# Mixed activations staged among the products of the tile ahead; last norms one tile later

## The chip, the cores and the metric

The kernel runs on one core of a Trainium2 chip, as one program. The metric is the device time of one execution in microseconds. A core has five engines that run side by side, each with its own queue in which work is done in order: TensorE (PE, matrix products, with weight loads shown apart as PEld), VectorE (DVE, elementwise work with two operands, reads the product banks), ScalarE (ACT, casts, activations with scale and bias), GpSimd (POOL, elementwise work, and the issue of some DMAs) and SyncE (SP, the issue of the other DMAs). Products land in PSUM banks; the rest of the data lies in SBUF tiles of 128 partitions.

## What is computed

One layer of a hybrid backbone over 17 tiles of 128 tokens (tile 0 the context, tiles 1 to 16 the latent tokens), width 1024, in float32. Cut to what the change touches:

```python
    h = rmsnorm(x, norm1_g) * (1 + scale1) + shift1
    z = h @ w_in
    ...
    mix = jnp.concatenate([o_a, o_b, o_c], axis=-1) @ w_out
    x = x + gate1 * mix
    h = rmsnorm(x, norm2_g) * (1 + scale2) + shift2
    x = x + gate2 * (jnp.square(jax.nn.relu(h @ w_ff1)) @ w_ff2)
    return rmsnorm(x, final_g)
```

o_a is a gated linear attention, o_b a convolution along rows of tokens, o_c a spatial gating.

## The kernel before, in words

Every large product is made as three products of split operands: a float32 value is cast to a short high part on ACT, and the low part is the difference of value and high part, by a subtract on DVE or POOL. `mm3` (L174) then issues high x high, high x low and low x high. One unit of `mm_units` (L134) is three such products of 512 columns for one of eight chunks of the contraction; a tile of the w_out stage has two halves of eight units, 48 products.

The phases in order: the first runs through the tiles upward (w_in, the attention's sums), the second downward from tile 16 (gates, attention output, gating, the convolution's input) and writes each tile's mixed activations to `mix_d[t]` in device memory. Then comes the w_out stage (`out_proj`, L754), from tile 16 down to tile 0. Then the first feed-forward product in two groups of eight latent tiles (`left_operand`, `right_operand`, `ff1_units`), and the second (`ff2_units`, `finish`), which runs over eight chunks of the hidden width and, within each, over the tiles in five blocks.

What `out_proj(t)` does before: it finishes the convolution work that tile t needs (`cq.finish(t)`, L760), takes a buffer `mt` and two for the parts, loads `mix_d[t]` (L766), casts on ACT (L767), subtracts on POOL (L768), loads the residual rows `x1`, and returns the sixteen units. At the end of each half (`done`) DVE multiplies the bank by the gate (L777) and adds the residual (L778); after the second half, POOL stores `x1`, ACT sums the squares (L782), `rstd_of` makes the root (DVE L160, POOL L161) and ACT multiplies (L784). The transposes and the second norm's scaling for that tile (`h2_half`, L797) are handed to the next tile as two items, after its twelfth and its sixteenth unit. For odd tiles `h2_pair` (L815) makes sums and differences of two tiles' results on DVE and stores them to `tb_d` through POOL.

`weave(units, items)` (L149) writes units and items alternately: an item with number n comes ahead of unit n. `ticks` puts one turn of the convolution queue after each unit: `ConvQueue` (L952) holds the tap passes of the convolution (62 for each group of tiles, a DVE pass each), hands them out by a credit of 5.3 a tile, and lists a norm and a silu step per tile as due some slots after the group's last tap. `finish(t)` runs turns at once until what tile t needs is written.

What is written first has the higher priority, but it is no strict order: the planner of the tile framework walks through all instructions when the kernel is built, keeps an estimate of when each is ready and a buffer free, and fixes each engine's queue by that. Products and transposes (`mm`, `tr`), taps and the loads through `ld_in_order` keep the order in which they are written. Buffers come from pools: `T` tiles (18 of 128 x 1024, pool `tp`, opened at L1143 where the buffers `hb` of phase two lay), `w` tiles (23, of which w_out's parts take 16), and for tile 16 the pair of `hunit`.

`right_operand` (L1151) loads one piece of a feed-forward operand from `tb_d`, by a DMA that POOL issues, and splits it in place with ACT and DVE (`split_in_place`, L1147: cast L1148, subtract L1149). It is called for 14 pieces per group of tiles (i from 0 to 6, kk 0 and 1).

In `finish` (L1377), at the last chunk, each half of a tile is multiplied by its gate, added to the residual and squared with a running sum on ACT; after the second half DVE adds the two sums, `rstd_of` makes the root, DVE scales both halves (L1392, recorded at L67) and SP stores them.

Of the kernel before, what the change touches and what calls it, by code (L numbers as in the profile page):

```python
# [8 lines left out]
F32 = mybir.dt.float32  # L9
# [11 lines left out]
NT = 17  # L21
# [22 lines left out]
def tile_hybrid(  # L44
# [12 lines left out]
    def x_rows(t):  # L57
        return x_prompt[0] if t == 0 else x_sample[0, (t - 1) * P:t * P, :]

    def y_rows(t):  # L60
        return y_prompt[0] if t == 0 else y_sample[0, (t - 1) * P:t * P, :]
# [49 lines left out]
    def wtile(dt=F32R):  # L111
        return wp.tile([P, D], dt, tag="w", name="w", bufs=23)

    def hunit():
        return hb.tile([P, 2, D], F32R, name="hb"), hb.tile([P, D], F32, name="hc")
# [15 lines left out]
    def ld_in_order(out, in_):  # L131
        tc.keep_in_program_order(ld.dma_start(out=out, in_=in_))
# [615 lines left out]
    def tunit(dt=F32R):  # L748
        return tp[0].tile([P, D], dt, tag="T", name="T", bufs=18)

    def gate_row(dst, g, cd):
        ld.dma_start(out=dst, in_=gate_d[g, cd:cd + 1].rearrange("o k p -> o (k p)").broadcast_to([P, D]))

    def out_proj(t):  # L754

        cd = 0 if t == 0 else 1
        if cd not in g1rows:
            g1rows[cd] = wtile(F32)
            gate_row(g1rows[cd], 0, cd)
        cq.finish(t)  # L760
        if t == NT - 1:
            hu, mt = hunit()
            mh, ml = hu[:, 0], hu[:, 1]
        else:
            mt, mh, ml = tunit(F32), tunit(), tunit()
        ld_in_order(out=mt, in_=mix_d[t].rearrange("p k t -> p (k t)"))  # L766
        S.copy(out=mh, in_=mt)  # L767
        G.tensor_tensor(out=ml, in0=mt, in1=mh.bitcast(F32), op=ALU.subtract)  # L768
        x1 = wtile(F32)
        ld_in_order(out=x1, in_=x_rows(t))  # L770

        tmp = xp_tile()[:, 0:D] if t == 0 else wtile(F32) if t == NT - 1 else tunit(F32)

        def done(half):
            def f(pz):
                fs = slice(half * 512, (half + 1) * 512)
                V.tensor_tensor(out=tmp[:, fs], in0=pz, in1=g1rows[cd][:, fs], op=ALU.mult)  # L777
                V.tensor_tensor(out=x1[:, fs], in0=tmp[:, fs], in1=x1[:, fs], op=ALU.add)  # L778
                if half == 1:
                    st.dma_start(out=x1_d[t], in_=x1)  # L780
                    ssq = const.tile([P, 1], F32, name="ssq3", bufs=2)
                    act(tmp, x1, AF.Square, accum_out=ssq)  # L782
                    rstd_of(ssq, ssq, D)
                    S.mul(tmp, x1, ssq)  # L784
            return f

        def lhs(k):
            ks = slice(k * P, (k + 1) * P)
            return mh[:, ks], ml[:, ks]

        units = []
        for half in range(2):
            units += mm_units(512, lhs, of_pairs(wo[half]), done(half))

        hs = []

        def h2_half(kq):  # L797
            pt = gbank()
            for kk in range(4):
                k = kq * 4 + kk  # L800
                tr(pt[:, kk * P:(kk + 1) * P], tmp[:, k * P:(k + 1) * P])
            hf = tmp.rearrange("p (k t) -> p k t", k=KD)
            for kk in range(4):
                k = kq * 4 + kk
                act(hf[:, k, :], pt[:, kk * P:(kk + 1) * P], AF.Identity, scale=s2[:, k, cd:cd + 1],
                    bias=modc[:, KD + k, cd:cd + 1])
            ks = slice(kq * 4, kq * 4 + 4)
            if t == 0:
                split(hc[0][:, ks], hc[1][:, ks], hf[:, ks])
            elif kq == 1:  # L810
                h2_pair(t, hf)

        return units, [(12, lambda: h2_half(0)), (16, lambda: h2_half(1))]
# [22 lines left out]
    def ticks(n, rate):  # L836
        return [(p_ + 0.5, lambda: cq.tick(rate / n)) for p_ in range(n)]
# [3 lines left out]
    with ExitStack() as p2:  # L841
# [293 lines left out]
                late = list(zip((8, 6), late2))  # L1135


        units, late3 = out_proj(NT - 1)
        weave(units, late + ticks(16, RATE3))


    hbs.close()
# [1 line left out]
    hc = []  # L1144
    TB = [{}, {}]

    def split_in_place(hi, lo):  # L1147
        S.copy(out=hi, in_=lo.bitcast(F32))  # L1148
        V.tensor_tensor(out=lo, in0=lo.bitcast(F32), in1=hi.bitcast(F32), op=ALU.subtract)  # L1149

    def right_operand(g, i, kk, dst):  # L1151

        unit = tunit if i < 4 else uunit
        hi, lo = unit(), unit()
        st.dma_start(out=lo.bitcast(F32).rearrange("p (k n) -> p k n", k=2), in_=tb_d[g][:, i, 2 * kk:2 * kk + 2])
        split_in_place(hi, lo)
        dst[i, kk] = (hi, lo)

    for t in range(NT - 2, -1, -1):
        units, nxt_late = out_proj(t)  # L1160
        if t == 0:
            hc += [tunit().rearrange("p (k t) -> p k t", k=KD) for _ in range(2)]
        items = late3 + ticks(16, RATE3)
        if t == 2:

            items += [(10 + 4 * kk, lambda kk=kk: right_operand(0, 0, kk, TB[0])) for kk in range(2)]
        weave(units, items)
        late3 = nxt_late
# [196 lines left out]
    def residual(t, y):  # L1365
# [8 lines left out]

        return half

    def finish(t, y):  # L1377

        ssq = const.tile([P, 2], F32, name="ssq4", bufs=4)
        tmp = raw()  # L1380

        def half(h, py):
            fs = slice(h * 512, (h + 1) * 512)
            V.tensor_tensor(out=tmp[:, fs], in0=py, in1=g2rows[min(t, 1)][:, fs], op=ALU.mult)  # L1384
            V.tensor_tensor(out=y[:, fs], in0=y[:, fs], in1=tmp[:, fs], op=ALU.add)  # L1385
            act(tmp[:, fs], y[:, fs], AF.Square, accum_out=ssq[:, h:h + 1])
            if h == 1:
                V.tensor_tensor(out=ssq[:, 0:1], in0=ssq[:, 0:1], in1=ssq[:, 1:2], op=ALU.add)  # L1388
                rstd_of(ssq[:, 0:1], ssq[:, 0:1], D)
                for i in range(2):  # L1390
                    fs = slice(i * 512, (i + 1) * 512)
                    stt(y[:, fs], y[:, fs], ssq[:, 0:1], fgr[:, fs], ALU.mult, ALU.mult)  # L1392
                    ld.dma_start(out=y_rows(t)[:, fs], in_=y[:, fs])

        return half

# [39 lines left out]
    for c in range(NC_):  # L1436
        w2n = []
        if c == NC_ - 2:
            g2rows[0] = tunit(F32)
            gate_row(g2rows[0], 1, 0)  # L1440
        for b in range(5):
            units = ff2_units(c, b, F, w2)
            items = []
            nb, ncx = (b + 1, c) if b < 4 else (0, c + 1)
            if ncx < NC_:
                F, steps = load_f(ncx, nb)
                items += zip((3.5, 9.5) if b < 4 else (0, 1), steps)
            if c + 1 < NC_ and b < 4:
                items.append((14.5, lambda f=(c + 1) * CF + b: w2n.append(load_ff2(f))))
            weave(units, items)  # L1450
        w2 = w2n
    tps.close()


# [27 lines left out]
```

## Time and profile before

| | |
|---|---|
| time, median of 3 runs | 2534.2 us (2531.51 to 2536.76) |
| the profiled execution: its time | 2536.06 us |
| the profiled execution: its span | 2534.3 us |
| PE busy | 2357.0 us, 93% of the span |
| DVE busy | 1500.6 us, 59% |
| ACT busy | 891.2 us, 35% |
| POOL busy | 432.3 us, 17% |
| mean granted TensorE clock | 0.968 of full speed |

The span runs from the first to the last instruction of the profile; the execution's own time also holds what lies around it. Busy shares are means over stages with different limits. A small helper such as `mm` or `act` gives its own line number to all that it issues, so instructions are told apart by their tiles (`out<-in`): products of the w_out stage are `z<-w,T`.

### The profile page before, as it was taken

Reading aid. Unit: us, or ns where it says so; the run is one execution under the profiler, and the core shown is the slowest. Engines: PE = TensorE matmul, PEld = TensorE weight load, DVE = VectorE, ACT = ScalarE, POOL = GpSimd, SP = SyncE. Lnnn points to the kernel's source line nnn. Section 1 sums busy time; section 2 is a strip of 40 time slices with the busy share of each in tenths; the row PEclk is TensorE's granted clock in tenths of the full one; section 3 lists DMA queues with packets and bytes.
Section 4 is the critical chain, followed back from the end, with each engine's and each line's share of the span. In section 5 each row is a group of like instructions: output and inputs, shape, how many; then the busy total and the mean of one; then the engine's idle time right before and its main releaser. Section 6 shows DMA issues by size and latency. Waiting matters only on the chain. (4 is left out here: it accounts for less than half of the span.)

```text
span 2534.3 us, 32290 instructions
## 1 busy us (share of the span) xinstructions
PE 2357.0 (93%) x12402; PEld 1920.9 (76%) x12402; DVE 1500.6 (59%) x2526; ACT 891.2 (35%) x1710; POOL 432.3 (17%) x593
## 2 busy tenths in 40 slices
PE   7999999999977778699999999999999999999996
PEld 5788886777755556478888778887888888888885
DVE  5987755878875663465555666665134344344886
ACT  4666764332434243443332433333321111011132
POOL 2332225444413233300000100000000000000000
PEclk9999999999988888799999999999999999999998
DMA  8655534433433435433222533334032122122442
GB/s 282 227 203 199 201 123 149 129 129 136 140 130 137 144 121 192 162 108 106 104 95 93 205 117 100 106 127 173 31 100 74 48 87 87 38 92 79 137 152 86
DMA packets 145323, 326.26 MB, mean 129 GB/s; under 512 B 13349, under 2 KB 58703, under 8 KB 141584
## 3 DMA queue, kind: packets, MB, share of 16 engines
q1 hardware_dynamic: 110640, 191.73, 23.1%
q0 software_dynamic: 34528, 132.46, 14.6%
q8 instruction: 98, 1.61, 0.3%
q14 instruction: 57, 0.47, 0.1%
HBM read 213.24 MB, written 110.90 MB: 128 GB/s over the span
## 5 line engine op out<-in xcount | busy, mean ns | idle before, releaser
L126 PE MATMUL z<-w,hb 128*128 128x512 f32 (+1 forms) x2438 | 552.1, 372 | 15.2 <-ACT hb L767 10.6
L126 PEld LDWEIGHTS z<-w,hb 128*128 128x128 f32 x2438 | 412.8, 192 | 92.6 <-ACT hb L767 10.8
L126 PE MATMUL z<-v,u 128*128 128x512 f32 x1224 | 304.3, 391 | 7.2 <-ACT u L1148 4.7
L126 PE MATMUL z<-T,v 128*128 128x512 f32 x1152 | 286.9, 401 | 15.6 <-ACT T L1148 6.4
L126 PE MATMUL g<-v,u 128*128 128x512 f32 x1224 | 300.9, 390 | 0.0
L126 PE MATMUL z<-w,T 128*128 128x512 f32 x768 | 213.3, 430 | 75.5 <-ACT T L767 51.4
L126 PEld LDWEIGHTS z<-v,u 128*128 128x128 f32 x1224 | 229.4, 188 | 60.7 <-DVE u L1149 8.5
L126 PEld LDWEIGHTS z<-T,v 128*128 128x128 f32 x1152 | 218.2, 191 | 70.3 <-ACT T L1148 7.7
L126 PE MATMUL z<-u,v 128*128 128x512 f32 x1152 | 269.8, 392 | 0.0
L126 PEld LDWEIGHTS g<-v,u 128*128 128x128 f32 x1224 | 230.8, 189 | 48.3
L1148 ACT CAST u<-u 128x1024 fp32r<-128x1024 f32 (+1 forms) x92 | 85.6, 938 | 484.4 <-DMA u<-f_d 360.7
L126 PEld LDWEIGHTS z<-u,v 128*128 128x128 f32 x1152 | 218.0, 189 | 46.9
L126 PEld LDWEIGHTS z<-w,T 128*128 128x128 f32 x768 | 152.2, 205 | 118.2 <-ACT T L767 53.5
L67 DVE SCALAR_TENSOR_TENSOR cacc<-xp,wd,cacc 128x512 f32<-128x512 f32 (+2 forms) x360 | 226.7, 683 | 0.0
L1149 DVE TENSOR_TENSOR u<-u 128x1024 fp32r<-128x1024 f32 (+1 forms) x92 | 99.1, 1082 | 114.1 <-ACT u L1148 91.3
L161 POOL TENSOR_TENSOR ssq<-ssq,mhalf 128x1 f32<-128x1 f32 x51 | 34.6, 679 | 773.7 <-DVE ssq L160 772.9
L1422 DVE TENSOR_TENSOR T<-z,T 128x512 f32<-128x512 f32 x102 | 70.4, 690 | 135.8 <-PE z L126 135.4
L172 DVE TENSOR_TENSOR v<-raw,v 128x1024 fp32r<-128x1024 f32 x88 | 107.2, 1220 | 64.0 <-PE z L126 60.2
L1422 DVE TENSOR_TENSOR T<-g,T 128x512 f32<-128x512 f32 x102 | 70.3, 689 | 124.9 <-PE g L126 124.9
L172 DVE TENSOR_TENSOR v<-cacc,v 128x1024 fp32r<-128x1024 f32 x64 | 78.3, 1224 | 86.6 <-PE z L126 86.6
L171 ACT CAST v<-raw 128x1024 fp32r<-128x1024 f32 x88 | 92.5, 1052 | 92.1 <-issue 55.4
L126 PE MATMUL z<-u 128*128 128x512 f32 x408 | 115.3, 391 | 0.0
(288 smaller groups left out, 3116.3 us busy)
## 6 DMA issues: line engine op xcount, KB each, us to landing
raw<-in_w_ff_dram SPq DMA_DIRECT2D x96, 512.0 KB
f_d<-xp POOLq DMA_DIRECT2D x64, 512.0 KB, 3.4
u<-f_d SPq DMA_DIRECT2D x64, 512.0 KB
raw<-in_w_mod_dram SPq DMA_DIRECT2D x32, 512.0 KB
hb<-hT_d POOLq DMA_DIRECT2D x15, 1024.0 KB, 5.6
hT_d<-hb POOLq DMA_DIRECT2D x13, 1024.0 KB, 6.8
ss_d<-ss POOLq DMA_DIRECT2D x34, 256.0 KB, 4.0
r<-ss_d SPq DMA_DIRECT2D x34, 256.0 KB
```

The costliest lines, as they stand in the source:

```text
L67: return V.scalar_tensor_tensor(out=out, in0=in0, scalar=scalar, in1=in1, op0=op0, op1=op1)
L126: tc.keep_in_program_order(T.matmul(out, lhsT, rhs, start=start, stop=stop, skip_group_check=read))
L161: G.tensor_tensor(out=out, in0=out, in1=mhalf[:, 0:out.shape[-1]], op=ALU.pow)
L171: order(S.copy(out=hi, in_=src))
L172: order(V.tensor_tensor(out=lo, in0=src, in1=hi.bitcast(F32), op=ALU.subtract))
L1148: S.copy(out=hi, in_=lo.bitcast(F32))
L1149: V.tensor_tensor(out=lo, in0=lo.bitcast(F32), in1=hi.bitcast(F32), op=ALU.subtract)
L1422: V.tensor_tensor(out=ya[t][:, hs], in0=py, in1=ya[t][:, hs], op=ALU.add)
```

## The change

The load, cast and subtract of the mixed tile move out of `out_proj(t)` into `stage(t)`, whose two parts are items among the units of tile t+1: the loads (with `cq.finish(t)`) ahead of unit 1, cast and subtract ahead of unit 7. The low part is made in the loaded buffer, so a tile takes two T buffers for it instead of three. Tiles 16 and 15 take their buffers from `hunit`. `right_operand` gives the subtract of kk = 1 to POOL; kk = 0 stays on DVE. In `finish` the sum of the two halves' squares, the root, the scaling and the stores of a tile are written after the first half of the next tile (after all others for the last).

```diff
+    staged = {}
+    def stage(t):
+        cq.finish(t)
+        if t >= NT - 2:
+            hu, mt = hunit()
+            mh, ml = hu[:, 0], hu[:, 1]
+        else:
+            mh, ml = tunit(), tunit()
+            mt = ml.bitcast(F32)
+        ld_in_order(out=mt, in_=mix_d[t].rearrange("p k t -> p (k t)"))
+        x1 = wtile(F32)
+        ld_in_order(out=x1, in_=x_rows(t))
+        staged[t] = mh, ml, x1
+        def convert():
+            S.copy(out=mh, in_=mt)
+            G.tensor_tensor(out=ml, in0=mt, in1=mh.bitcast(F32), op=ALU.subtract)
+        staged[t, 0] = convert
+    def stages(t):
+        return [(1.0, lambda: stage(t)), (7.0, lambda: staged[t, 0]())] if t >= 0 else []
     def out_proj(t):
...
-        cq.finish(t)
-        if t == NT - 1:
-            hu, mt = hunit()
-            mh, ml = hu[:, 0], hu[:, 1]
-        else:
-            mt, mh, ml = tunit(F32), tunit(), tunit()
-        ld_in_order(out=mt, in_=mix_d[t].rearrange("p k t -> p (k t)"))
-        S.copy(out=mh, in_=mt)
-        G.tensor_tensor(out=ml, in0=mt, in1=mh.bitcast(F32), op=ALU.subtract)
-        x1 = wtile(F32)
-        ld_in_order(out=x1, in_=x_rows(t))
+        mh, ml, x1 = staged[t]
...
+        stage(NT - 1)
+        staged[NT - 1, 0]()
         units, late3 = out_proj(NT - 1)
-        weave(units, late + ticks(16, RATE3))
+        weave(units, late + ticks(16, RATE3) + stages(NT - 2))
...
-    def split_in_place(hi, lo):
+    def split_in_place(hi, lo, eng=V):
         S.copy(out=hi, in_=lo.bitcast(F32))
-        V.tensor_tensor(out=lo, in0=lo.bitcast(F32), in1=hi.bitcast(F32), op=ALU.subtract)
+        eng.tensor_tensor(out=lo, in0=lo.bitcast(F32), in1=hi.bitcast(F32), op=ALU.subtract)
...
-        split_in_place(hi, lo)
+        split_in_place(hi, lo, G if kk else V)
...
-        items = late3 + ticks(16, RATE3)
+        items = late3 + ticks(16, RATE3) + stages(t - 1)
...
+    norms = []
     def finish(t, y):
...
+            if h == 0 and norms:
+                norms.pop()()
             if h == 1:
-                V.tensor_tensor(out=ssq[:, 0:1], in0=ssq[:, 0:1], in1=ssq[:, 1:2], op=ALU.add)
-                rstd_of(ssq[:, 0:1], ssq[:, 0:1], D)
-                for i in range(2):
-                    fs = slice(i * 512, (i + 1) * 512)
-                    stt(y[:, fs], y[:, fs], ssq[:, 0:1], fgr[:, fs], ALU.mult, ALU.mult)
-                    ld.dma_start(out=y_rows(t)[:, fs], in_=y[:, fs])
+                norms.append(norm)
+        def norm():
+            V.tensor_tensor(out=ssq[:, 0:1], in0=ssq[:, 0:1], in1=ssq[:, 1:2], op=ALU.add)
+            rstd_of(ssq[:, 0:1], ssq[:, 0:1], D)
+            for i in range(2):
+                fs = slice(i * 512, (i + 1) * 512)
+                stt(y[:, fs], y[:, fs], ssq[:, 0:1], fgr[:, fs], ALU.mult, ALU.mult)
+                ld.dma_start(out=y_rows(t)[:, fs], in_=y[:, fs])
...
         w2 = w2n
+    norms.pop()()
     tps.close()
```

## Rows read from the trace of the kernel before

**Rows 1.** Windows, pairs of tiles: length; busy PE, PEld, DVE, ACT, POOL; clock.

```profile
761.29:800.24 38.95, 27.83 (x123) 21.63 (x123) 20.78 (x43) 16.84 (x35) 14.69 (x16) 0.85 0.42 149
800.24:836.53 36.29, 28.29 (x118) 21.91 (x118) 21.75 (x37) 15.63 (x33) 12.46 (x13) 0.88 0.36 127
836.53:873.58 37.05, 27.71 (x113) 21.48 (x113) 23.00 (x31) 12.37 (x24) 11.92 (x12) 0.87 0.42 135
873.58:910.43 36.85, 28.00 (x112) 21.62 (x113) 21.96 (x35) 12.37 (x24) 11.48 (x12) 0.87 0.42 136
910.43:948.09 37.66, 27.80 (x124) 21.92 (x124) 24.78 (x72) 17.03 (x36) 14.46 (x18) 0.86 0.34 112
948.09:985.76 37.67, 27.55 (x121) 21.46 (x121) 17.41 (x37) 17.32 (x37) 14.25 (x17) 0.86 0.45 143
...
1021.48:1058.07 36.59, 27.46 (x113) 21.21 (x113) 9.76 (x15) 12.53 (x25) 11.28 (x12) 0.87 0.25 80
```

**Rows 2.** Waits of PE in the stage: us in total, times, longest.

```profile
PE z L126 <- ACT T L767: 51.4, 8, 8.8
PE z L126 <- POOL T L768: 24.1, 15, 2.3
```

**Rows 3.** Timeline of ACT: start, us, engine, line, operation, out<-in.

```profile
871.44 1.15 ACT L784 ACTIVATE T<-w,ssq 128x1024 f32<-128x1024 f32 x1 [1.03 <-POOL ssq L161]
872.50 1.03 ACT L767 CAST T<-T 128x1024 fp32r<-128x1024 f32 x1
```

**Rows 4.** Timeline of PE, one pair of tiles; in brackets the idle time before.

```profile
876.97 10.79 PE L126 MATMUL z<-w,T 128*128 128x512 f32 x34 [2.17 <-POOL T L768]
...
893.22 8.20 PE L126 MATMUL z<-w,T 128*128 128x512 f32 x34 [1.33 <-POOL T L768]
...
904.49 0.60 PE L129 MATMUL g<-ident,T 128*128 128x128 f32 x4
```

**Rows 5.** Windows of the same pair's two tiles; the granted clock is the third last number.

```profile
873.50:888.50 15.00, 12.75 (x43) 9.72 (x43) 7.43 (x8) 0.23 (x2) 3.40 (x3) 0.69 0.47 141
888.50:905.20 16.70, 15.26 (x71) 11.90 (x69) 11.25 (x21) 7.62 (x17) 4.82 (x4) 1.00 0.38 127
```

**Rows 6.** Timelines of PE and DVE at the end.

```profile
2508.40 0.84 PE L126 MATMUL g<-u 128*128 128x512 f32 x3
...
2513.84 0.84 PE L126 MATMUL g<-u 128*128 128x512 f32 x3
...
2521.47 0.68 DVE L1384 TENSOR_TENSOR raw<-g,T 128x512 f32<-128x512 f32 x1
...
2524.77 1.41 DVE L67 SCALAR_TENSOR_TENSOR T<-T,ssq,cacc 128x512 f32<-128x512 f32 x2 [0.75 <-POOL ssq L161]
```

**Rows 7.** Waits of DVE in the last chunk, from 2421 us on.

```profile
DVE T L67 <- POOL ssq L161: 10.1, 16, 0.8
DVE ssq L1388 <- ACT raw L64: 10.0, 15, 0.8
```

**Rows 8.** Waits of DVE in one pair of tiles, 836.53 to 873.58.

```profile
DVE ssq L160 <- ACT T L64: 2.6, 2, 1.3
DVE T L827 <- ACT T L64: 0.8, 1, 0.8
```

**Rows 9.** Timelines of PE and ACT, one norm of the convolution.

```profile
914.41 0.63 PE L129 MATMUL g<-ident,cacc 128*128 128x128 f32 x2
...
916.83 0.56 ACT L64 ACTIVATE raw<-g,mv 128x256 f32<-128x256 f32 x1 [6.45 <-issue]
```

**Rows 10.** Line L1149: durations ns (least, median, most), first and last start.

```profile
L1149 DVE TENSOR_TENSOR T<-T x16: 1214/1224/1226, 1014.1 to 1457.9; 128x1024 fp32r<-128x1024 f32 x16
```

**Rows 11.** Line L1155 (loads by POOL) in the fill, 1055 to 1100.

```profile
DMA to landing us min/median/max: 7.7/12.3/14.4
```

**Rows 12.** Timelines of DVE and POOL, 872 to 877.

```profile
872.70 4.78 DVE L67 SCALAR_TENSOR_TENSOR cacc<-xp,wd,cacc 128x512 f32<-128x512 f32 x3
...
874.57 2.35 POOL L768 TENSOR_TENSOR T<-T 128x1024 fp32r<-128x1024 f32 x1
```

## The prediction

> **What bounds the kernel now.** I read in this order: the slices of the page, where TensorE (PE) is below nine tenths only in the first slice and from the 12th to the 17th; the busy time of each pair of tiles in this second place, the w_out stage; PE's waits there; PE, ACT, POOL and DVE in order of time; then the chain that ended last, which lies on DVE for the final 100 us. Everywhere else PE is close to full, so the change is worth what PE idle time and slow PE time it removes, and the tail.
>
> The w_out stage (tiles 15 to 0) runs from 761.29 to the next stage's first product at 1058.07 [rows 1]. Inside it PE waits for two things only: the cast of the mixed tile (L767, eight times, 51.4 us) and the low part's subtract on POOL (L768, fifteen times, 24.1 us) [rows 2]. The cast waits for no data: it stands in ACT's queue behind the multiply L784 of the tile just finished, and starts as that ends (871.44 + 1.15, then 872.50) [rows 3]. So for every second tile the chain is last product, eviction, square, root, multiply, cast, two products, subtract, rest. A third loss follows: after the wait 34 products took 10.79 us, in the pair's other tile 8.20 us [rows 4]; the granted clock was 0.69 in that stretch, a mix of the levels of 1.2 and 2.4 GHz, and 1.00, the upper one, in the next, where PE had been at work before [rows 5]. Eight times about 2.4 us is 19 us. Together 51 + 24 + 19 = 94 us.
>
> At the end the last products run from 2513.84 to 2514.68, but DVE finishes the last tile only at 2524.77 + 1.41 = 2526.18 [rows 6]. In that last chunk DVE stands still 10.1 us for POOL's power and 10.0 us for ACT's sum of squares, once each per tile [rows 7].
>
> **The change part by part.**
>
> *Mixed tiles staged one tile ahead.* Cast and subtract of tile t-1 are now written after seven of the sixteen units of tile t, so they stand ahead of tile t's second eviction, square and multiply in the queues. Both are ready when the tile's load has landed, and PE needs them some 6 us later. Removed from PE's path: both waits, and the cold clock behind them. What is late next? A tile without waits is 46 products and 8 transposes from 893.22 to 904.49 + 0.60, 11.87 us, plus two products at 0.24: 12.35 us, 24.7 a pair [rows 4]. DVE's work per pair is 20.8, 21.8, 23.0, 22.0, 24.8 and 17.4 us, less in the last two [rows 1]. DVE works in order, and in a pair it also stands 2.6 us for the sum of squares and 0.8 for the pair's first sum [rows 8]; where convolution norms run (pairs 1, 2, 5 and 6) I add 2.2 us, an estimate from the 3.0 us that a norm takes from its transposes at 914.41 to the end of ACT's normalising at 916.83 + 0.56 [rows 9], shared among three engines. That gives DVE 26.4, 27.4, 26.4, 25.4, 30.4 and 23.0. Taking the larger of DVE and PE: 26.4 + 27.4 + 26.4 + 25.4 + 30.4 + 24.7 + 24.7 + 24.7 = 210 us for sixteen tiles. Today it is 296.8 less the 5.5 us between the last transposes and the next stage's first product, which stay: 291.3. To this comes the wait ahead of tile 15, whose start lies 5.8 us after the end of tile 16. So 291.3 + 5.8 - 210 = 87 us. The ceiling, PE alone, is 8 x 24.7 and 4 us of convolution transposes, 202, which is 95 us.
>
> Against that, three small terms. (1) Tile 14's staging is the first to take slots of the new pool `tp` while tile 15 still sits in the old hb buffers. If its slot lies over those, the load waits for tile 15's last product, and its flight (which no row shows alone; taken as up to 5 us), cast and subtract follow: at most 8 us once, otherwise nothing; I take 3. (2) `cq.finish` is called most of a tile sooner. By the queue's own arithmetic (0.662 credits for a tap of four tiles, 5.3 a tile) the taps of tiles 1 to 4 end in tile 8 as before, and only the last two silu steps, of tiles 2 and 1, are forced early, in tile 5, directly behind tile 1's norm: PE can wait the 3.0 us of [rows 9] less the unit between: 0 to 3, taken as 2. (3) Tile 16's load now goes out on SP ahead of the gate row instead of behind it: 0 to 2 us gained, taken as 1. The staged loads are the same two DMAs per tile on SP; behind one that waits for its slot stand only the next loads. Each tile now takes three slots of T instead of four, so slots come free sooner. Sum for the stage: 87 - 3 - 2 + 1 = 83 us.
>
> *Half of right_operand's subtracts to POOL.* Fourteen of them: 1.22 us on DVE [rows 10] becomes 2.35 on POOL (a subtract of this shape, [rows 12]), while DVE does the other half at the same time. One stands in tile 2, six in the fill of the feed-forward stage, seven at its change of group. Where PE waits for just this operand it loses 1.1 us; where it waited behind DVE's queue it gains 1.2. Bounds: 14 x 1.13 = 16 us lost, to 3 us gained; the loads that feed the fill land 12.3 us after issue [rows 11], so most of it is hidden behind them: 2 us lost. POOL's queue also issues these loads; that is the last rival.
>
> The Trainium skill speaks against this part. "SBUF — State Buffer", section "Who interferes with whom", says that a DVE instruction with two SBUF inputs and a GpSimd instruction that reads SBUF exclude each other. The row agrees: three taps took 4.78 us, where three passes of this shape at 0.68 [rows 6] are 2.0, with POOL's subtract inside [rows 12]. By that rule the shift frees no DVE time; what it does to the staged tiles is rival (b), worked out there from the rows.
>
> *Last norms one tile later.* The norm of a tile is now written after the first half of the next, so DVE no longer waits for the square just issued: of 20.1 us of standing [rows 7] half or more goes. DVE's work per tile there is four passes of 0.68, two of one column and 1.41, some 4.5 us, 5.2 with one wait left, against PE's 5.44 (2508.40 to 2513.84) [rows 6], so PE becomes the bound. The last half still has its chain, from 2521.47 to 2526.18, 4.7 us [rows 6]; it can start at 2514.9, or at 2516 if tile 1's norm is just ahead. The end moves from 2526.2 to between 2519.6 and 2520.7: 5.5 to 6.6 us, taken as 5.5. The output's last landing behind it stays.
>
> Sum: 83 - 2 + 5.5 = 86.5 us. The profiled execution took 2536.1 us (span 2534.3), so 2449.6; it lies 0.07% above the median of 2534.2, and I forecast **2449 us**.
>
> **The rivals.** (a) *PE alone is the bound*: DVE fills its standing time with taps, as the planner may order them otherwise. For it: the warm tiles of today run at PE's pace with a full share of taps. Against: waits of 1.3 us for the squares recur in every tile. 95 + 5.5: 2436 us.
> (b) *DVE falls behind through POOL.* From a tile's end to the end of its multiply lie about 5.4 us (the mean wait of 6.4 us [rows 2] less the cast's 1.03 [rows 3]); its transposes stand after twelve units, 8.7 us. If the staged subtract holds the second eviction for 2.35 us [rows 12] and stands ahead of the power on POOL for as long again, this is 10.1 and PE stalls, 1.4 to 2.4 us in each of the 11 tiles where DVE is nearly full: 15 to 26 us. At the upper end 2449 + 26 = 2475 us. For it: DVE's margin is under 1 us a tile. Against: the subtract is ready before the eviction in most tiles.
> (c) *The staging is not early*: the load waits for slots, or the planner leaves the cast behind the multiply. Then only POOL's 24 us go, with the end's 5.5 less 2: 2508 us. Against: ACT has work for less than half the stage, and loads need fewer slots now.
> (d) *Slower*: on POOL each new subtract waits for a cast that waits for a load. If the planner sets it ahead of the next load's issue, loads go one by one: 12.3 us landing [rows 11], 1.03 cast and 2.35, 15.7 us for each of 13 operands, up to 204 us: 2449 + 204 = 2653 us. It decides from six operands on (six times 15.7 is 94, over the 88 gained elsewhere). Against: the issues wait for no data that POOL makes, so they should go first.
>
> **How the numbers follow.** Forecast (2440 to 2460) 0.48, (a) 0.15, (b) 0.25, (c) 0.08, (d) 0.04. The range covers the forecast, (a) and (b), with the unknown ends of the fill (14 more) and of tile 14: 2434 to 2488; (c), (d) and a little stay out. A measurement of this kernel tells about 0.2% (5 us) from no change. Only (d) is slower; a mild form of it, or (c) with the full loss of 16 us, could end near no change. Faster 0.94, same 0.02, slower 0.04.
>
> **What would show it.** Right: no wait of PE for the cast in the stage and few for POOL; a granted clock near 1.00 from tile 15 on; some 215 us from tile 15's first product to the next stage's; DVE's busy share in it over 0.8 up to tile 5; at the end DVE's last pass some 6 us behind PE's last product. Wrong: PE waiting for the new cast or subtract (c); PE waiting for the multiply ahead of the transposes (b); long gaps between POOL's loads of tb_d (d); a stage still over 240 us.

## The result, and the profile after

The changed kernel takes 2472.9 us (median of 4 runs, 2469.2 to 2478.2) against 2533.3 us in the same set: ratio 0.9762, 95% interval 0.9738 to 0.9785. It is faster, by 60 us; the forecast was 2449 us, a gain of 86.5. The four runs fall into two pairs, 2469.2 and 2470.0 us, and 2475.8 and 2478.2 us; the profile is of the 2475.8. The profiled execution has a span of 2474.1 us (2534.3 before), 60.2 us less, and it is this difference that is taken apart here.

The page after, busy time first, then PE and its granted clock in 40 slices:

```profile
PE 2341.6 (95%) x12402; PEld 1913.3 (77%) x12402; DVE 1518.3 (61%) x2512; ACT 890.6 (36%) x1710; POOL 470.2 (19%) x607
...
PE   6999999999989988799999899999999999999996
...
PEclk9999999999989999799999899999999999999998
```

Of the dip of PE from the 12th to the 17th slice there remain the 12th (tile 16's start), the 15th to 17th (the convolution's norm, the stage's end and the fill), none under 7; there is a new one in the 23rd, at the change of group. What PE waits for from tile 16's first product to the first feed-forward products (725 to 990 us: us in total, times, longest):

```profile
PE g L129 <- ACT raw L64: 9.2, 2, 8.8
PE z L126 <- ACT hb L771: 7.5, 1, 7.5
PE g L129 <- ACT T L799: 7.5, 5, 3.0
PE z L126 <- ACT v L171: 5.3, 1, 5.3
PE z L126 <- ACT T L771: 3.6, 1, 3.6
PE z L126 <- POOL hb L772: 1.5, 1, 1.5
PE z L126 <- POOL T L772: 1.5, 1, 1.5
```

The cast (51.4 us before) and the subtract (24.1) of [rows 2] are gone but for one wait each at tile 14; tile 16's own (`hb`), which lie ahead of the windows of [rows 2], stay. New are the waits for the convolution's norm (`raw`) and for the multiply L799 ahead of the transposes. The same waits in PE's timeline (start, us, in brackets the idle time before):

```profile
734.15 1.22 PE L126 MATMUL z<-w,hb 128*128 128x512 f32 x2 [7.53 <-ACT hb L771]
...
767.61 1.22 PE L126 MATMUL z<-w,T 128*128 128x512 f32 x2 [3.60 <-ACT T L771]
770.31 2.08 PE L126 MATMUL z<-w,T 128*128 128x512 f32 x4 [1.48 <-POOL T L772]
...
808.18 1.12 PE L129 MATMUL g<-ident,T 128*128 128x128 f32 x4 [3.00 <-ACT T L799]
...
902.23 0.69 PE L129 MATMUL g<-ident,raw 128*128 128x128 f32 x2 [8.82 <-ACT raw L64]
902.57 9.60 PE L126 MATMUL z<-w,T 128*128 128x512 f32 x33
...
984.09 5.12 PE L126 MATMUL z<-T,v 128*128 128x512 f32 x12 [5.30 <-ACT v L171]
```

Four stretches hold what changed. They are read from the timelines of every run's profile, and the experiments are compared by them too. "Stage" runs from tile 16's first product to the first `z<-T,v`, "fill" from there to the first `g<-v,T` x24, "change" (the change of group) from the start of the last `z<-u,v` block of the first group to the start of the first one of the second, "tail" from the end of PE's last product to the end of DVE's last pass. All four are in us and of one execution each; the times are medians, and each ratio is to the kernel before as measured beside it. In the last two kernels tile 16's first product can't be told from those ahead of it, so their stage is left open.

| kernel | us | ratio to before (95%) | stage | fill | change | tail |
|---|---|---|---|---|---|---|
| before | 2533.3 | | 319.7 | 43.6 | 30.5 | 11.5 |
| the change | 2472.9 | 0.976 (0.974 to 0.979) | 249.9 | 49.6 | 39.2 | 11.6 |
| ro_only | 2547.8 | 1.005 (1.003 to 1.006) | 321.8 | 49.8 | 36.3 | 11.5 |
| ro_dve | 2456.1 | 0.969 (0.968 to 0.970) | 244.3 | 43.6 | 31.6 | 11.7 |
| ro_sp | 2451.7 | 0.967 (0.966 to 0.969) | 247.0 | 39.7 | 31.5 | 11.6 |
| norm_old | 2475.1 | 0.976 (0.975 to 0.977) | 249.2 | 47.9 | 39.0 | 11.4 |
| norm_kept | 2466.1 | 0.973 (0.971 to 0.974) | 247.7 | 48.1 | 40.2 | 6.0 |
| silu_own | 2463.4 | 0.972 (0.970 to 0.973) | 236.7 | 47.8 | 39.8 | 11.5 |
| sub_dve | 2462.6 | 0.971 (0.970 to 0.972) | 238.3 | 49.9 | 40.1 | 11.5 |
| combo | 2445.1 | 0.965 (0.963 to 0.966) | 238.5 | 43.5 | 30.9 | 6.0 |
| combo_sub | 2432.2 | 0.959 (0.958 to 0.961) | 226.2 | 42.8 | 30.9 | 6.0 |
| best_sp | 2417.1 | 0.953 (0.952 to 0.955) | 226.0 | 38.2 | 22.6 | 6.0 |
| best_s16 | 2404.0 | 0.948 (0.947 to 0.950) | | 38.1 | 22.8 | 6.0 |
| best_half | 2415.8 | 0.954 (0.952 to 0.955) | | 39.9 | 32.3 | 6.0 |

For the change: stage 69.8 us shorter and its start 4.2 us earlier (738.35 to 734.15), together 74 against 83 forecast; fill and change 5.9 and 8.7 us longer, 14.6 against 2; tail 0.1 longer against 5.5 shorter; the rest 0.9 better. 74.0 - 14.6 - 0.1 + 0.9 = 60.2.

### The profile page after: what moved, and what is told of

Its sections match the earlier page's. It is cut to its first block, busy times and chain, and to the rows that moved or that the text cites. A ratio compares the mean times of both kernels' runs of the same rounds, so it can differ in the third digit from the quotient of the medians.

```text
span 2474.1 us, 32304 instructions
## 1 busy us (share of the span) xinstructions
PE 2341.6 (95%) x12402; PEld 1913.3 (77%) x12402; DVE 1518.3 (61%) x2512; ACT 890.6 (36%) x1710; POOL 470.2 (19%) x607
## 3 DMA queue, kind: packets, MB, share of 16 engines
q0 software_dynamic: 34528, 132.46, 15.1%
## 4 chain that ended last, share of the span: by engine, by line
PE 62%; DVE 12%; issue 4%; DMA 4%; ACT 3%; POOL 3%; POOLq 0%; SPq 0%; DVEq 0%; ACTq 0%
PE z L126 42%; PE g L126 19%; DVE cacc L67 5%; DMA T<-tb_d 1%; PE g L129 1%; DMA u<-f_d 1%; DVE T L67 1%; DVE u L1166 1%; DVE T L1404 1%; DVE raw L1403 1%; POOL ssq L161 1%; DVE uv L67 1%; DVE w L793 1%; ACT T L64 1%; ACT raw L64 1%
## 5 line engine op out<-in xcount | busy, mean ns | idle before, releaser
L126 PE MATMUL z<-w,hb 128*128 128x512 f32 (+1 forms) x2486 | 563.0, 373 | 13.5 <-ACT hb L771 7.5
L126 PEld LDWEIGHTS z<-w,hb 128*128 128x128 f32 x2486 | 420.8, 192 | 92.9 <-ACT hb L771 7.8
L126 PEld LDWEIGHTS g<-v,u 128*128 128x128 f32 x1224 | 230.5, 188 | 48.1
L67 DVE SCALAR_TENSOR_TENSOR cacc<-xp,wd,cacc 128x512 f32<-128x512 f32 (+2 forms) x360 | 237.6, 713 | 0.0
L126 PE MATMUL z<-w,T 128*128 128x512 f32 x720 | 183.5, 409 | 5.2 <-ACT T L771 3.6
L126 PEld LDWEIGHTS z<-w,T 128*128 128x128 f32 x720 | 136.3, 194 | 35.9 <-ACT T L771 3.8
L1166 DVE TENSOR_TENSOR u<-u 128x1024 fp32r<-128x1024 f32 (+1 forms) x86 | 91.8, 1073 | 102.8 <-ACT u L1165 102.5
```

Of the source, the lines that this page charges most:

```text
L67: return V.scalar_tensor_tensor(out=out, in0=in0, scalar=scalar, in1=in1, op0=op0, op1=op1)
L126: tc.keep_in_program_order(T.matmul(out, lhsT, rhs, start=start, stop=stop, skip_group_check=read))
L1166: eng.tensor_tensor(out=lo, in0=lo.bitcast(F32), in1=hi.bitcast(F32), op=ALU.subtract)
```

## The experiments

Each is the changed kernel with the edit shown, except ro_only, which is the kernel before. The theory formed from the traces: three losses in three places, each in an order of instructions and not in the work itself (for the change of group the last run shows otherwise); the rivals stand with each run.

**Where fill and change of group lose.** In the kernel before, POOL issues the loads of `tb_d` one behind the other (start, us):

```profile
1061.01 0.53 POOL L1155 DMA_DIRECT2D T<-tb_d  x1
1061.53 0.53 POOL L1155 DMA_DIRECT2D u<-tb_d  x1
1062.30 0.53 POOL L1155 DMA_DIRECT2D T<-tb_d  x1 [0.25 <-DMA tb_d<-T]
```

POOL's timeline after:

```profile
987.16 0.53 POOL L1172 DMA_DIRECT2D T<-tb_d  x1
1000.41 2.44 POOL L1166 TENSOR_TENSOR T<-T 128x1024 fp32r<-128x1024 f32 x1 [12.72 <-ACT T L1165]
1002.80 0.57 POOL L1172 DMA_DIRECT2D u<-tb_d  x1
1003.37 0.54 POOL L1172 DMA_DIRECT2D T<-tb_d  x1
1003.92 2.37 POOL L1166 TENSOR_TENSOR u<-u 128x1024 fp32r<-128x1024 f32 x1
1006.23 0.58 POOL L1172 DMA_DIRECT2D u<-tb_d  x1
```

Before, the sixth and seventh issue follow the fifth at once; after, the sixth stands behind a subtract that waits 12.7 us for the cast of an earlier load. But the subtract is also slower on POOL, and DVE stands beside it. Three kernels ask which of these it is, and a fourth, best_half at the end, is needed for the answer.

```diff
 # ro_dve
-        split_in_place(hi, lo, G if kk else V)
+        split_in_place(hi, lo)
```

> The changed kernel with all subtracts of right_operand back on DVE. Theory: in the changed kernel the fill of the first feed-forward stage took 5.9 us more than before (49.5 against 43.6) and the change of group 9.1 us more (48.7 against 39.6), because POOL, which issues these loads, now puts a subtract that waits for its load between two issues, and DVE stands beside POOL's subtract. Then the whole 15 us come back: 2458 us, 0.994 of the changed kernel's 2473. Rival A, the estimate in the prediction: the shift costs 2 us, and the longer fill has another cause (the stage ends earlier relative to the stores to tb_d): 2471 us. Rival B: what costs is the lock of DVE beside POOL in the staged tiles too, then nothing is seen here but the one operand in tile 2: 2472 us.

2456.1 us: fill and change are back at 43.6 and 31.6. The cause is in the shift, not in the staging. The stage is 5.6 us shorter too: 1.7 us were PE's wait at 962.5 for a multiply in tile 2, behind the subtract of the first operand (POOL, 957.88 to 960.30), and 3.3 us are the clock that these two executions met, not the edit (last section).

```diff
 # ro_only, on the kernel before
...
-        split_in_place(hi, lo)
+        split_in_place(hi, lo, G if kk else V)
```

> The kernel before, with nothing of the change but its second part: right_operand's subtract of kk = 1 on POOL. Theory (POOL issues these loads, and a subtract that waits for its own load stands between two issues): the loss at the fill and at the change of group is there without the staging, 6 + 8.7 us, so 2548 us, 1.006 of the kernel before. Rival: it comes only with the staging, which brings the fill closer to the stores of tb_d: 2535 us, no difference. Rival of the prediction: the subtracts are hidden, 2 us: 2536 us.

2547.8 us against 2535.6, ratio 1.0047 (1.0034 to 1.0060): a small difference, but clear of noise. Alone, this part makes the kernel slower by 12 us, 6.2 in the fill and 5.8 at the change.

```diff
 # ro_sp
-        st.dma_start(out=lo.bitcast(F32).rearrange(...), in_=tb_d[g][:, i, 2 * kk:2 * kk + 2])
+        ld.dma_start(out=lo.bitcast(F32).rearrange(...), in_=tb_d[g][:, i, 2 * kk:2 * kk + 2])
```

> The changed kernel, half of right_operand's subtracts on POOL as in the change, but the loads of tb_d issued by SyncE, where no subtract stands ahead of them. It tells the two causes of the 15 us at the fill and at the change of group apart. Theory (the loads wait in POOL's queue behind subtracts that wait for earlier loads): most of it comes back, 2461 us, with a fill of about 45 us and 32 us between the last two product blocks around the change of group. Rival (POOL's subtract is just slower, 2.35 against 1.22 us, and DVE stands beside it): nothing comes back, 2473 us. A third: on SyncE's queue the loads stand behind weight loads that wait for a buffer, and it is slower than 2473.

2451.7 us. POOL has its subtracts as in the change, and still the change of group is back at 31.5 and the fill at 39.7, shorter than before the change: SyncE issues the fill's first two loads at 971.8 and 972.3, ahead of the first feed-forward product at 978.9. It looks as if it had been the queue alone. But what the subtract itself costs is still there, in the timelines of PE, DVE and POOL at the change of group:

```profile
1370.91 2.19 PE L126 MATMUL z<-T,v 128*128 128x512 f32 x6 [2.91 <-DVE T L1166]
1376.79 2.50 PE L126 MATMUL z<-T,v 128*128 128x512 f32 x5 [3.69 <-POOL T L1166]
...
1371.72 5.58 DVE L1228 TENSOR_TENSOR cacc<-raw,cacc 128x512 f32<-128x512 f32 x1
...
1372.09 2.36 POOL L1166 TENSOR_TENSOR u<-u 128x1024 fp32r<-128x1024 f32 x1
1374.40 2.34 POOL L1166 TENSOR_TENSOR T<-T 128x1024 fp32r<-128x1024 f32 x1
```

A DVE pass that takes 0.68 us in the kernel before took 5.58 with two subtracts inside, and PE waited for DVE and then for POOL. So the loads' move to SyncE must have gained something else there, and the kernel before shows what it can be: a store `f_d<-xp` that waits 8.1 us for DVE stands in POOL's queue ahead of the loads, with no subtract on POOL at all.

```profile
1444.17 0.54 POOL L1250 DMA_DIRECT2D f_d<-xp  x1 [8.10 <-DVE xp L67]
1444.70 0.53 POOL L1155 DMA_DIRECT2D u<-tb_d  x1
```

The Trainium skill would have pointed to it: "DMA: Bandwidth & Descriptors", section "SWDGE vs HWDGE vs iDMA", gives plain transfers to SyncE or ScalarE and leaves to GpSimd those that accumulate, cast or are irregular. ro_sp agrees for these loads (21.2 us faster than the change), and so does best_sp below (15.1 us faster than combo_sub).

**The convolution's steps.** In the change, the silu of tile 1 is written ahead of unit 1 of tile 5, right behind the norm of the same tile. DVE, then ACT, of that norm:

```profile
895.77 0.42 DVE L894 BATCH_NORM_STATS2 bst<-g 128x6 f32<-128x256 f32 x1
...
898.85 0.15 DVE L67 SCALAR_TENSOR_TENSOR mv<-mv 128x1 f32<-128x1 f32 x1
```

```profile
900.58 1.15 ACT L799 ACTIVATE T<-w,ssq 128x1024 f32<-128x1024 f32 x1 [1.22 <-POOL ssq L161]
901.63 0.55 ACT L64 ACTIVATE raw<-g,mv 128x256 f32<-128x256 f32 x1
```

Its transposes were done at 892.1; the statistics start only at 895.77, behind ten taps, a sum and an eviction, and the normalising at 901.63, behind the tile's multiply, though its factors had been ready since 899.0. That is 10 us, where the prediction took the 3.0 of [rows 9].

```diff
 # silu_own
                         for j, (f, g) in enumerate(norms):
-                            self.due += [(self.slot + 9 + 10 * j, tiles, f), (self.slot + 21 + 10 * j, tiles, g)]
+                            own = tiles[-1 - j:][:1]
+                            self.due += [(self.slot + 9 + 10 * j, own, f), (self.slot + 21 + 10 * j, own, g)]
```

> The changed kernel with one edit in the convolution queue: a norm or silu step that is due counts for its own tile alone, not for its whole group, so that the staging of tile 4 no longer forces the last two silu steps right behind the norm of tile 1 (they are written ahead of units 2 and 12 of tile 5 instead of both ahead of unit 1). Theory: the one wait of 8.8 us at 893.4 goes, and most of the slow clock behind it (33 products in 9.6 us, some 1.5 us over a warm stretch): 9 to 10 us, 2463 us. Rival: DVE and ACT are behind by as much there, and the wait turns up at the next transposes: 2473 us, no change. In between: the norm's chain of 10 us hides behind eleven units (7.5 us) only in part, 2466 us.

2463.4 us. PE's wait for the norm there is 1.16 us instead of 8.82, and PE stays at speed behind it: 12 products in 3.03 us (0.25 each), where 33 had taken 9.60 (0.29 each). Its stage is 13.2 us shorter, but 3.5 of these are the clock again and not the edit (last section). Its timeline:

```profile
899.12 0.44 PE L129 MATMUL g<-ident,raw 128*128 128x128 f32 x2 [1.16 <-ACT raw L64]
...
899.75 3.03 PE L126 MATMUL z<-w,T 128*128 128x512 f32 x12
```

**The staged subtract.** Rival (b) of the prediction said that POOL's subtract holds DVE and so makes the multiply late. After the change, DVE and POOL beside each other:

```profile
797.10 3.05 DVE L793 TENSOR_TENSOR w<-T,w 128x512 f32<-128x512 f32 x1
800.08 2.73 DVE L67 SCALAR_TENSOR_TENSOR cacc<-xp,wd,cacc 128x512 f32<-128x512 f32 x4
...
803.45 0.69 DVE L793 TENSOR_TENSOR w<-T,w 128x512 f32<-128x512 f32 x1
```

```profile
797.19 2.40 POOL L772 TENSOR_TENSOR T<-T 128x1024 fp32r<-128x1024 f32 x1
```

The same add takes 0.69 us alone and 3.05 with the subtract inside: POOL's 2.40 us are taken from DVE whole (0.69 + 2.40 = 3.09).

```diff
 # sub_dve
-            G.tensor_tensor(out=ml, in0=mt, in1=mh.bitcast(F32), op=ALU.subtract)
+            V.tensor_tensor(out=ml, in0=mt, in1=mh.bitcast(F32), op=ALU.subtract)
```

> The changed kernel with the staged subtract of all seventeen tiles on DVE (1.22 us each) instead of POOL (2.35 us). Theory (a DVE pass with two SBUF operands stands still beside POOL's subtract, so POOL takes the longer time from DVE anyway): DVE wins about 1.1 us a tile in the ten tiles where the taps run, the stalls ahead of the transposes (7.5 us in five waits) fall by half and the 3.6 + 1.5 us at tile 14 shrink a little: 2468 us. Rival: POOL's subtract runs beside DVE for most of its time, and DVE is the bound in these tiles, so it gets up to 1.2 us more for each of eleven: 2486 us.

2462.6 us, 10 us faster, twice the expectation: giving work to the engine that seemed full made the stage 11.6 us shorter. PE's waits in it (725 to 973 us), of those in question:

```profile
PE g L129 <- ACT raw L64: 6.6, 1, 6.6
...
PE g L129 <- ACT T L799: 2.0, 1, 2.0
```

The waits for the multiply fall from 7.5 us in five to one of 2.0, the wait for the norm from 8.8 to 6.6, and tile 14's for the subtract is gone. The one that is left, in tile 2, stands behind a subtract that this edit leaves on POOL, that of the first feed-forward operand; in the change its like was 1.7 of the 7.5 us. The rule of the Trainium skill cited in the prediction ("SBUF — State Buffer", section "Who interferes with whom") agrees with the add of 3.05 us.

**The late norms.** DVE's waits after the change, from 2380 us on, and its last tile but one and its end:

```profile
DVE T L67 <- POOL ssq L161: 9.7, 15, 0.8
DVE ssq L1412 <- ACT raw L64: 9.3, 14, 0.8
```

```profile
2456.15 0.69 DVE L1404 TENSOR_TENSOR T<-T,raw 128x512 f32<-128x512 f32 x1
2457.63 0.16 DVE L1412 TENSOR_TENSOR ssq<-ssq 128x1 f32<-128x1 f32 x1 [0.79 <-ACT raw L64]
...
2458.74 0.75 DVE L67 SCALAR_TENSOR_TENSOR T<-T,ssq,cacc 128x512 f32<-128x512 f32 x1 [0.75 <-POOL ssq L161]
2459.41 0.68 DVE L1403 TENSOR_TENSOR raw<-z,T 128x512 f32<-128x512 f32 x1
...
2464.57 1.41 DVE L67 SCALAR_TENSOR_TENSOR T<-T,ssq,cacc 128x512 f32<-128x512 f32 x2 [0.75 <-POOL ssq L161]
```

The norm (L1412) still stands right behind its own tile's last add, ahead of the next tile's first multiply (L1403): it is written later but not queued later, and the waits are those of [rows 7].

```diff
 # norm_old
-            if h == 0 and norms:
-                norms.pop()()
             if h == 1:
-                norms.append(norm)
+                norm()
...
-    norms.pop()()
```

> The changed kernel with the norms of the last chunk as before. Theory: the new place of the norm did nothing, since in the changed kernel DVE still stands 0.79 us for ACT's sum and 0.76 us for POOL's power once a tile, and its last pass ends 11.6 us behind PE's last product (11.5 before): 2473 us, within 2. Rival, the prediction: the shift is worth 5.5 us, and something else in the last chunk took them: then it is slower without it, 2478 us.

2475.1 us, ratio 0.9761 where the change has 0.9762: this part did nothing that can be told from noise.

```diff
 # norm_kept: the passes keep the order written; root() = sum and root of a tile, scale() = its scaling and stores
...
+            kept(V.tensor_tensor(out=tmp[:, fs], in0=py, in1=g2rows[min(t, 1)][:, fs], op=ALU.mult))
+            if h == 1 and norms:
+                norms.pop()()      # scale() of the tile before
+            kept(V.tensor_tensor(out=y[:, fs], in0=y[:, fs], in1=tmp[:, fs], op=ALU.add))
             act(tmp[:, fs], y[:, fs], AF.Square, accum_out=ssq[:, h:h + 1])
             if h == 0 and norms:
-                norms.pop()()
+                norms.pop(0)()     # root() of the tile before
             if h == 1:
-                norms.append(norm)
+                norms.extend((root, scale))
...
```

> The changed kernel with the norm of the last chunk truly later: DVE's passes there keep the order in which they are written, the sum and the root's argument of a tile stand behind the next tile's first add, its scaling behind the next tile's second multiply. Theory: the planner, which fills DVE's queue by its own estimate of what is ready first, had drawn the late norm forward to the very square it waits for; with the order kept DVE's work per tile (4.2 us) lies under PE's 5.4, only the last tile's chain follows PE's last product (some 5 us instead of 11.5): 6 us faster than the changed kernel, 2467 us, and DVE ends about 5 us behind PE. Rival: POOL's power and ACT's square are late anyway, so DVE still ends 11 us behind PE: 2473 us. Other rival: the kept order makes DVE wait for PE's banks with scaling work queued behind it, and PE is held: 2476 us or more.

2466.1 us, 6.8 less than the change. DVE now waits for PE, and ends 2455.55 + 1.41 - 2451.01 = 5.95 us behind PE's last product. Its waits from 2380 us on:

```profile
DVE raw L1404 <- PE g L126: 10.3, 11, 1.0
DVE T L67 <- POOL ssq L1418: 1.1, 3, 0.8
DVE ssq L1415 <- ACT raw L64: 0.8, 1, 0.8
```

**Together.** combo joins the edits of ro_dve, silu_own and norm_kept; combo_sub adds that of sub_dve; best_sp adds that of ro_sp, and best_s16 this:

```diff
 # best_s16, among the items of tile 0 in phase two
+                    items += [(10.4, lambda: stage(NT - 1)), (19.0, lambda: staged[NT - 1, 0]())]
...
-        stage(NT - 1)
-        staged[NT - 1, 0]()
```

> Three of the edits in one kernel: staging as in the change, right_operand's subtracts all on DVE, steps of the convolution queue due for their own tile alone, order of the last norms kept. If the causes lie in different places their gains add: 17 + 9.5 from the two measured alone, and 6 expected of the norms, so 2473 - 32.5 = 2440 us. Rival: the first two gains overlap (both take load from DVE or POOL around tiles 6 to 2): 2447 us.

2445.1 us, 5 more than the sum. Fill, change and tail have their whole gains; the stage, 238.5, is no shorter than silu_own's. Of ro_dve's 5.6 us in the stage only the 1.7 at tile 2 can be put down to the edit, and that wait is gone in combo too. Against silu_own combo then loses 3.4 us to the clock: from tile 16's first product to the wait at 836 its execution took 101.6 us, silu_own's 98.3 (last section).

> The kernel before this one in the list, with the staged subtract on DVE as well. Theory (the waits ahead of the transposes come from POOL's subtract, which holds DVE and the power's place in POOL's queue): what is left of these waits goes, some 6 us, and part of tile 14's: 2433 us. Rival: the 10.5 us that this edit gave alone were the same silu wait (8.8 there, 6.6 with it) and the clock behind it, so no more than 3 us are left to gain: 2438 us.

2432.2 us: with the silu steps apart, the subtract on DVE still makes the stage 12.3 us shorter, so its gain was not the silu wait; about 3 of these can be the clock, since combo's execution was of the slower kind.

> combo_sub, with right_operand's loads issued by SyncE as well (all its subtracts on DVE). In ro_sp the fill took 39.7 us, less than the 43.6 of the kernel before and the 42.8 of combo_sub, since POOL's queue holds other work ahead of the loads. Theory: 3 us at the fill come on top: 2429 us. Rival: what was gained there came from sharing the subtracts between POOL and DVE once the loads were free, so nothing is gained with all of them on DVE: 2432 us.

2417.1 us, 15 less than combo_sub instead of 3. The expectation missed the change of group, which goes from 30.9 to 22.6 us, close to the 22.5 from block to block ahead of it: nearly all of its waits are hidden once neither POOL's queue nor its subtract stands in the way. (One of 1.3 us for DVE turns up in the block behind it.) In the profiled executions another 4.0 us lie ahead of the stage, within what that start varies by in all these kernels (731.8 to 737.9).

> best_sp, and tile 16 staged as all others are: its loads ahead of unit 11 of the last tile of phase two and its cast and subtract ahead of unit 19, instead of both behind that tile. Theory: the wait of 8 us of PE for the cast at 734, the one of 1.1 to 1.5 us for the subtract and the slow clock behind them (6.5 us for 16 products, 3.9 warm) go: 11 us, 2418 us. Rival: the parts of w_out for that tile, or the convolution's last inputs, are the next to be late, and half of it stays: 2424 us.

2404.0 us (2401.8 to 2407.0), ratio 0.9484 (0.9471 to 0.9497): the fastest. PE goes over into tile 16 without the wait for the cast, the one for the subtract stays at 1.16, and the 16 products behind it take 3.99 us instead of 6.50:

```profile
731.82 6.27 PE L126 MATMUL z<-w,hb 128*128 128x512 f32 x26
739.26 3.99 PE L126 MATMUL z<-w,hb 128*128 128x512 f32 x16 [1.16 <-DVE hb L772]
```

The last kernel takes the edit of ro_dve out of best_s16 again.

> best_s16 (2404 us) with half of right_operand's subtracts on POOL as in the change, the loads still issued by SyncE. It asks what sharing the subtracts is worth once no load stands behind them. Theory: a subtract takes 2.4 to 3.4 us on POOL in ro_sp (1.2 on DVE) and PE waits for it, so nothing is gained: the fill grows by 1 to 2 us, the change of group by 3 to 4 (in ro_sp PE stood 2.9 us for DVE and 3.7 us for POOL there), 2409 us. Rival: half the work for DVE shortens the fill, 2401 us.

2415.8 us, 12 slower: 1.9 in the fill, 9.5 at the change. Half of the subtracts on POOL is a loss even where no load stands behind them.

This corrects the reading of ro_sp. Fill and change of the four kernels that have both choices:

| fill / change, us | loads issued by POOL | loads issued by SyncE |
|---|---|---|
| subtracts all on DVE | 43.6 / 31.6 (ro_dve) | 38.1 / 22.8 (best_s16) |
| half of them on POOL | 49.6 / 39.2 (the change) | 39.9 / 32.3 (best_half) |

The right column has the other edits too, but they are not what makes it differ: combo_sub, with these edits and the loads on POOL, has 42.8 / 30.9. In the fill the shift costs 6.0 us with the loads on POOL and 1.9 without: two thirds of that loss were the queue. At the change of group it costs 7.6 us with the loads on POOL and 9.5 without: there the subtract on POOL is by itself enough for the whole loss, whatever issues the loads. ro_sp came back to 31.5 because the loads' move gained there about what the subtracts cost. How much of this cost is the subtract's own 2.4 us and how much the time that DVE stands beside it was not tried.

## Why the prediction was right and where it was wrong

The time fell within the range and the sign is right: the staging, the largest part, works as the prediction said. But 26 us of the forecast gain are missing: 9 in the stage, 12.6 in fill and change, 5.6 in the tail, less 0.9 elsewhere. That the time lies next to 2475 us, the upper end of rival (b), is luck: of (b)'s mechanism there was about 8 us. Two signs that the prediction had named point at what was missed: PE waits for the multiply ahead of the transposes, its sign of (b), and POOL's fifth and sixth load stand 15.6 us apart (987.16 and 1002.80), its sign of (d).

- *Staging removes the waits for cast and subtract, and with them the slow clock*: right. Of 94 us counted in the stage, PE still waits 5.1 us, at tile 14; the granted clock is 1.00 in the windows without a long wait (824 to 878 us, 928 to 953).
- *Tile 14, 3 us*: 5.1 us. The price was about right, its reason was not: the load went out at 746.90, before tile 15 had begun. The cast came at 766.51, in ACT's queue behind tile 16's second scaling and a norm. Which of these held it was not tried.
- *The forced silus, 2 us, at most 3*: the worst sized term of the stage, 8.8 us and 1.7 behind it (33 products in 9.60 us, where 36 took 8.62 at 796.56 in the same execution). [rows 9] shows a norm that met idle queues; this one stood behind taps, evictions, a store's issue and a multiply. What stands ahead in DVE's, POOL's and ACT's queue was read off another tile's norm.
- *DVE as the bound, 8 us over PE alone*: the size held, by another way. DVE's time went in part into standing beside POOL's subtract, which made the multiply late five times: four times by the staged subtract (5.8 us, and 2.3 of slow clock behind the first: 12 products in 5.39 us, 3.05 in ro_dve), and once, at tile 2, by the subtract of an operand (1.7). That is rival (b), of which the forecast had said "Against: the subtract is ready before the eviction in most tiles"; sub_dve, where the four are gone, shows that it mattered.
- *Tile 16's load ahead of the gate row, 1 us*: the first product comes 4.2 us earlier in these two executions, but ten kernels with this load order have it between 731.8 and 737.9 (two with the old: 737.8 and 738.4). PE's wait for the cast there tells more: 7.4 to 9.0 us in the ten, 10.6 and 10.2 in the two. Some 1 to 3 us; the rest of the 4.2 is scatter.
- *Half of right_operand's subtracts on POOL, 2 us*: 14.6 us. The step that failed is "most of it is hidden behind the loads". In the fill (6.0 us) it takes the loads' issue for granted: two thirds of the loss are rival (d) in a mild form, to which 0.04 was given on the ground that "the issues wait for no data that POOL makes, so they should go first". The planner set subtracts between them; (d) had one load at a time, here they went out in ones and twos. At the change of group (7.6 to 9.5 us) the subtract's own cost is not hidden: for the seven operands there the prediction's bound of 1.13 us each, with nothing hidden, is 7.9 us, and best_half has 9.5 with no load behind a subtract.
- *Last norms, 5.5 us*: nothing. The step that failed is that what is written later is queued later. The trace shows the norm where it was before; why the planner put it there is not shown. The working behind the term was sound: with the order kept the tail is 5.95 us, 5.6 shorter, where 5.5 to 6.6 was worked out.
- Two small slips: PE is below nine tenths in the last slice before too (6), which the first paragraph leaves out and the part on the end takes up; and 2449.6 us, taken 0.07% down to the median, are 2448.

## What to carry to other kernels

When an operation moves to an engine that also issues loads, read that engine's queue and not only its busy share: a subtract that waits for one load holds every issue behind it. An edit that gives a loss back need not have removed its cause: it can have gained as much elsewhere, and only all four pairings of two choices tell. Work whose whole time is taken from a full engine anyway, as POOL's subtract was from DVE here, is cheaper on the full engine itself, if it takes half the time there. And under a planner, writing an instruction later can move nothing; look where it stands in the queue of the trace, and keep the order where it matters.

## What the runs showed of the hardware

- A load's issue takes POOL 0.53 to 0.58 us and SyncE 0.32 to 0.45 in most cases (fill of the change, and ro_sp).
- One DVE pass and one POOL subtract, both on SBUF data, took their times one after the other: 3.05 us for an add of 0.69 beside a subtract of 2.40 (the change), 5.58 us for one of 0.68 beside two of 2.36 and 2.34 (ro_sp).
- The same order of instructions meets different clocks. Seven kernels have the same instructions in PE's, DVE's, ACT's and POOL's queue from tile 16's first product to the wait at 836. Near 767 us, after the same wait of 3.6 us, two products took 1.22 us in four of them (the change, norm_old, ro_sp, combo) and 0.72 or 0.73 in three (ro_dve, norm_kept, silu_own); the granted clock was 0.50 there in the change and 1.00 in ro_dve, the levels of 1.2 and 2.4 GHz. In the first kind the next wait ahead of transposes, at 808, was 2.9 to 3.0 us, and the products behind it were slow (clock 0.50 from 808.2 to 814.1 in the change); in the second kind it was 1.4 to 1.5 us, and they were not (1.00 from 806.3 to 812.2 in ro_dve). The way from tile 16's first product to the wait at 836 took 100.3 to 101.8 us against 98.3 to 98.5. What decides between the two is not shown. Differences of the stage of up to 3.5 us between two single profiles mean nothing here. ro_dve, for the lines of the change further up:

```profile
765.95 0.73 PE L126 MATMUL z<-w,T 128*128 128x512 f32 x2 [3.61 <-ACT T L771]
...
806.28 0.66 PE L129 MATMUL g<-ident,T 128*128 128x128 f32 x4 [1.45 <-ACT T L799]
```
